# Where matmul operands lie modulo 256 bytes: one place for all moving and stationary tiles, and 64 and 192 bytes from it for the gates' weights

## The chip, the core and the metric

The kernel runs on one core of one Trainium2 chip. The metric is device time in microseconds. Before the change the median of three runs is 1592.05 us (1591.93 to 1592.51). TensorE is called PE, its weight loads PEld, VectorE DVE, ScalarE ACT, GpSimd POOL.

## The reference

One layer of a decoder trunk, 512 tokens, width 2048, float32. Conditioning gives shift, scale and gate; the normalised input goes through one wide projection; its parts feed a latent attention of 16 heads and a chunked gating unit; both are gated, added and projected back.

```python
mod = c_act @ w_ada[l] + b_ada[l]
shift, scale, gate = jnp.split(mod, 3, axis=-1)
h = rmsnorm(x, attn_norm_g[l]) * (1.0 + scale[:, None]) + shift[:, None]
proj = h @ w_in[l]
q_lat, kv_lat, k_rope, z_mla, u, v, z_sgu, g_mla, g_sgu = split_cols(proj, IN_SPLITS)
q = (rmsnorm(q_lat, q_norm_g[l]) @ w_uq[l])      # 16 heads of 128 + 64 rotary
kv = (rmsnorm(kv_lat, kv_norm_g[l]) @ w_ukv[l])  # 16 heads: keys 128, values 128
y_mla = causal_mla_attention(q_nope, q_rope, k_nope, k_rope, v_mla) * jax.nn.silu(z_mla)
y_sgu = chunked_causal_sgu(u, v, sgu_norm_g[l], w_spatial[l], b_spatial[l]) * jax.nn.silu(z_sgu)
merged = jax.nn.sigmoid(g_mla) * y_mla + jax.nn.sigmoid(g_sgu) * y_sgu
x = x + gate[:, None] * (merged @ w_out[l])
return rmsnorm(x, final_norm_g)
```

## The kernel before

Every large product is made of three matmuls. A float32 operand is split into a high part (ACT copies it into the type float32r) and a low part (DVE subtracts the high part), and `mm3` (L135) adds high·high (L136), high·low (L137) and low·high (L138). A matmul has a stationary operand of 128 x 128, which a weight load brings into the array, and a moving operand of 128 rows and up to 512 columns. Both are read from SBUF, where a tile has the same address in all partitions. Where a tile starts modulo 256 bytes is called its place here.

The stages, in order:

- Latents (11 to 156 us): the query and key-value latents and three columns of the last head. A stream of weights passes through three raw buffers; `Stream.split_to` (L90) splits each of them into the pairs w0h, w0l and w1h, w1l in turn. Stationary: w. Moving: h, the normalised input, transposed, 16 tiles of high and low parts, 512 columns. A weight gives 24 matmuls.
- v (156 to 340 us): v and the shared rotary key. Stationary: h. Moving: w, 512 columns twice, then 384 twice and 320.
- Gates (351 to 1117 us): z, g, u, s and t (the five gate-like projections) of head pairs. Two products are computed as seven smaller ones, in the manner of Winograd's form of Strassen's algorithm, from sums of weights and of input tiles (s1, s2, s4 are such sums, s3 goes back into h). A slot is one of these: eight column blocks of three matmuls with 256 moving columns (L1255 high·high, L1256 high·low, L1257 low·high), 24 in all, 266 slots. Stationary: w0, w2, w1 in turn, where w0 and w1 are the stream's buffers and w2 (with the raw buffers raw4 to raw7) lies in a pool `c1` on the other side of SBUF. Moving: h, or s1, s2, s4. A planner places ACT, DVE and transfer work of the slots by costs; it budgets 2.53 us of DVE for a slot. Some sums of weights are made by transfers that add while they land; POOL issues those (L636).
- Attention (1117 to 1400 us): for each head query, key and value products from the latents (w stationary for queries and keys with 512 columns, w moving for values with 256), scores, softmax, transposes and the product with the values.
- Output (1400 to 1581 us): merged tiles (b high, g low) stationary, w_out moving with 512 columns; six weights of the last column group are kept as dh and dl; the last block is cut into two of 256 columns.

What sets the places before: the stream's pair tiles are longer than the weights by `HALF` = 16 words, and the caller's `off` says by how much the high part is shifted (the low part gets `HALF - off`). Constants ahead of them in the pool, an `edge` tile on the right side, and `gap` tiles ahead of s1 and behind s4 shift the rest. In the slots' `split` (L651 to L654) the low part alone is shifted by 16 words in w0 and w1, and nothing in w2.

Of the kernel before, what the change touches and what calls it, by code (L numbers as in the profile page):

```python
# [11 lines left out]
F32 = mybir.dt.float32  # L12
F32R = mybir.dt.float32r
# [3 lines left out]
ALU = mybir.AluOpType  # L17
# [3 lines left out]
P = 128  # L21
# [6 lines left out]
SCALE = 1.0 / math.sqrt(192.0)  # L28
NEG = -1.0e30
GW = 1024  # L30
HALF = 16
TYPES = "zgust"


# [25 lines left out]
class Stream:  # L60
# [9 lines left out]
        self.n_dma = self.n_split = 0  # L70
        self.before = {}

    def add(self, ap, n, to=None, off=HALF):
        self.src.append((ap, n, to, off))
        return len(self.src) - 1

# [14 lines left out]
    def split_to(self, i):  # L91
        i = min(i, len(self.src) - 1)
        while self.n_split <= i:
            k = self.n_split
            self.dma_to(k)
            _, n, to, off = self.src[k]
            raw = self.raw.pop(k)
            self.n_split += 1
            if to is not None:
                hi, lo = to()  # L100
            else:
                pool, tag = self.parts[self.next_part]
                self.next_part = (self.next_part + 1) % len(self.parts)
                hi, lo = (pool.tile([P, GW + HALF], F32R, tag=tag + e, name=f"{tag}{e}_{k}")[:, o:o + GW]
                          for e, o in (("h", off), ("l", HALF - off)))
            self.nc.scalar.copy(hi[:, :n], raw[:, :n])  # L106
            self.nc.vector.tensor_tensor(out=lo[:, :n], in0=raw[:, :n], in1=hi[:, :n].bitcast(F32), op=ALU.subtract)  # L107
            self.hl[k] = (hi, lo)
# [8 lines left out]
def trunk_layer(ctx, tc, xT, xn, c, vecs, pos, wada, w1, w2, wv, wv3, wv4, wh, wh15, wq, wqr, wk, wvv, wo, wsT, bsp, gfin, out,  # L117
                dbg=None):
    nc = tc.nc
# [15 lines left out]
    def mm3(ps, ah, al, bh, bl, start, stop):  # L135
        PE.matmul(ps, ah, bh, start=start, stop=False)  # L136
        PE.matmul(ps, ah, bl, start=False, stop=False)  # L137
        PE.matmul(ps, al, bh, start=False, stop=stop)  # L138
# [5 lines left out]
    def pool(name, side=LEFT, **kw):  # L144
        return tc.tile_pool(name=name, bufs=1, side=side, reuse_waits="tile", **kw)
# [11 lines left out]
    def nt(p, shape, dt, tag, **kw):  # L157
        uid[0] += 1
        return p.tile(shape, dt, tag=tag, name=f"{tag}_{uid[0]}", **kw)

    def bcast(src, n):
# [4 lines left out]
    cst = ctx.enter_context(pool("cst"))  # L166
    wp = ctx.enter_context(pool("w"))
    edge = ctx.enter_context(pool("edge", side=RIGHT))
    nt(edge, [P, 24 + HALF], F32, "edge")
    latp = Scope("lat", side=RIGHT)  # L170
    ws = Stream(nc, [(wp, f"wraw{i}") for i in range(3)], [(wp, f"w{i}") for i in range(2)])

# [6 lines left out]
    DVE.memset(one, 1.0)  # L179
    ident = nt(cst, [P, P], F32, "ident")  # L180
    make_identity(nc, ident)
    tri = nt(cst, [P, P], F32, "tri")
    nc.gpsimd.memset(tri, 1.0)
    nc.gpsimd.affine_select(out=tri, in_=tri, compare_op=ALU.is_ge, fill=0.0, base=0,
                            pattern=[[1, P]], channel_multiplier=-1)
    ones = nt(cst, [P, P], F32R, "ones")
    DVE.tensor_copy(ones, one.broadcast_to([P, P]))
    eps = nt(cst, [P, 1], F32, "eps")
# [45 lines left out]
    gq, gr, gk, gvv = {}, {}, {}, {}  # L234
    c1 = [None]
# [2 lines left out]
    gr[0] = ws.add(wqr[0], 768)  # L238
    gq[0] = ws.add(wq[0], 768)
    gk[0] = ws.add(wk[0], 512)  # L240
    gvv[0] = ws.add(wvv[0], 1024, off=0)
    for h in range(1, H):
        gq[h] = ws.add(wq[h], 768)
        if h % 2 == 1 and h + 1 < H:
            gr[(h + 1) // 2] = ws.add(wqr[(h + 1) // 2], 768)
        gk[h] = ws.add(wk[h], 512)
        if h % 2 == 0:
            gvv[h // 2] = ws.add(wvv[h // 2], 1024, off=0)
    dp = [None]
    dlast = []  # L250

    def last_tiles():
        k = len(dlast)
        dlast.append((nt(dp[0].p, [P, GW], F32R, f"dh{k}"),
                      nt(dp[0].p, [P, GW + (HALF if k == 5 else 0)], F32R, f"dl{k}")[:, :GW]))
        return dlast[-1]

    go = {}
    for cg in range(3):
        for i in range(8):  # L260
            go[cg, i] = ws.add(wo[cg, i], GW, off=0)
            if cg == 2 and i < 6:
                go[3, i] = ws.add(wo[3, i], GW, to=last_tiles)
    for i in (6, 7):
        go[3, i] = ws.add(wo[3, i], GW, off=0)
    pend = []

    def get(i, ahead=1, run=1):
        r = ws.get(i, ahead)
        fs, pend[:] = pend[:run], pend[run:]  # L270
        for f in fs:
            f()
        return r
# [11 lines left out]
    def bank():  # L285
        n_bank[0] += 1
        return bank_at(ring[(n_bank[0] - 1) % len(ring)])
# [49 lines left out]
    hh, hl, hx = [None] * KC, [None] * KC, [None] * KC  # L337
# [32 lines left out]
    for q, sl in enumerate(quarters):  # L370
# [4 lines left out]
                            pattern=[[-1, P]], channel_multiplier=1)  # L375
# [26 lines left out]
    def dot_to(n):  # L402
        nonlocal n_dot
        while n_dot < min(n, KC):
            ada_dot(n_dot)
            n_dot += 1
# [82 lines left out]
    def store(dst, src):  # L489
        made.append((dst, src))  # L490
# [20 lines left out]
    for cg, w in enumerate(VW):  # L511
        psv = [bank()[:, :w] for _ in range(4)]
        for i in range(8):
            g = cg * 8 + i
            wH, wL = get(gv[g], ahead=1)
            if g < 8:
                fix_to(FIXED[KC + g], lambda: dot_to(DOTS[KC + g]))
            for k in range(2):
                j = 2 * i + k
                sl = slice(k * w, (k + 1) * w)  # L520
                for n in range(NB):
                    tk = slice(n * P, (n + 1) * P)
                    mm3(psv[n], hh[j][:, tk], hl[j][:, tk], wH[:, sl], wL[:, sl], j == 0, j == KC - 1)
            for j in gate_step.get(g, ()):
                ada_dot(2 * KC + j)
            if g == 31:
                ada.close()
                c1[0] = Scope("c1", side=RIGHT)
                sums["s4"] = nt(c1[0].p, [P, 8, 2, 256], F32R, "s4")
                nt(c1[0].p, [P, HALF], F32, "gap")  # L530
                sums["s4h"], sums["s4l"] = sums["s4"][:, :, 0], sums["s4"][:, :, 1]
            for f in early.pop(g, ()):
                f()
            stores()
        if cg == 0:
            xp.close()
            s12 = Scope("s12")
            nt(s12.p, [P, HALF], F32, "gap")
            for n in ("s1h", "s1l", "s2h", "s2l"):
                sums[n] = nt(s12.p, [P, 8, 256], F32R, n)  # L540
            tb = Scope("tB")

        def evac_v(n, cg, ps):
            m = VW[cg] // P
            w, c0 = m * P, sum(VW[:cg])
            junk = nt(tb.p, [P, S], F32, f"t{n % 2}") if cg == 0 else nt(latp.p, [P, S], F32, f"lat{10 + n % 2}")
            ACT.activation(junk[:, :w], ps[:, :w], AF.Square, accum_out=ssv[:, n, cg:cg + 1])
            t = nt(tb.p, [P, S], F32, "sig", bufs=2)
            ACT.copy(t[:, :VW[cg]], ps[:, :VW[cg]])
            store(v_d[n][:, c0:c0 + w], t[:, :w])  # L550
            if cg == 4:
                store(kr_d[n], t[:, w:VW[cg]])

        for n in range(NB):
            pend.append(lambda n=n, cg=cg, ps=psv[n]: evac_v(n, cg, ps))
# [63 lines left out]
    base = [slot_of[k][1] for k in range(n_pairs)]  # L619
# [27 lines left out]
    def add(k, q, r):  # L647
        tt(raws[k, q], raws[k, q], raws[k, r], ALU.add)

    def split(s):  # L650
        p, k = order[s]  # L651
        src = raws[k, {1: 11, 6: 11, 2: 11, 4: 11, 3: 12, 7: 22, 5: 21}[p]]
        pl, tag = parts[s % 3]
        own = pl is wp  # L654
        hi = nt(pl, [P, GW + (HALF if own else 0)], F32R, tag + "h")[:, :GW]
        lo = nt(pl, [P, GW + HALF], F32R, tag + "l")[:, HALF if own else 0:][:, :GW]
        split_of[s] = hi, lo
        ACT.copy(hi, src)  # L658
        return hi, lo, src
# [417 lines left out]
    used, s_, n = [s_bias] * 3, s_bias + 1, 0  # L1077
# [136 lines left out]
    for s in range(-4, 0):  # L1214
        done[0] = s
        if s % 2 == 0:
            half = (s + 4) // 2
            wH, wL = get(gz[half], ahead=1 if half == 0 else 0, run=0)
        for f in pend[:2]:
            f()  # L1220
        del pend[:2]
        if s == -1:
            while pend:
                pend.pop(0)()
            tb.close()
            mis = Scope("more")
            sg[0] = Scope("sgu")
        run(s, FIRST, EVAC, GATE)
        if s == -4:
            plain = bank_at(plain_bank)  # L1230
        for k in range(4):
            j = (s + 4) * 4 + k
            sl = slice(j % 8 * P, (j % 8 + 1) * P)
            mm3(plain, wH[:, sl], wL[:, sl], hh[j], hl[j], j == 0, j == KC - 1)
        run(s, SPLIT, BACK, MISC, LOAD)
        stores()
# [342 lines left out]
    for n in range(NB):  # L1579
# [16 lines left out]
        y, o = yt[:, n], 1536 + o  # L1596
# [80 lines left out]
```

## Time and profile before

| | before |
|---|---|
| median of three runs | 1592.05 us |
| profiled execution | 1591.48 us, span 1589.8 us |
| PE busy | 1575.8 us, 99% of the span, 10728 matmuls |
| PEld busy | 1462.7 us, 92% |
| DVE, ACT, POOL busy | 72%, 47%, 6% |
| TensorE clock granted | 1.00 nearly throughout |
| gates, 351 to 1117 us | 6384 of the matmuls, PEld busy 99% |

A matmul is pipelined: the next one starts before it ends, so the durations in the rows (277 ns, say) are longer than the time from start to start. In the timeline the first column is an instruction's start in us from the start of the span, the second its duration. In a table of stretches the columns are named in its first row. In a group of instructions (the page's fifth part) the columns are line, engine, operation, output<-inputs (moving, then stationary), shapes, count | busy us, mean ns | idle time ahead and what ended it.

### The profile page before, as it was taken

The numbers are of one execution on the slowest core, as the hardware profiler recorded it, in microseconds if no ns is written. First come the engines' busy times: TensorE is split into PE (matmuls) and PEld (weight loads), VectorE is DVE, ScalarE is ACT, GpSimd is POOL, SyncE is SP. The second block draws the span as 40 slices with busy tenths as digits, with TensorE's granted clock in tenths as the row PEclk, the third lists the DMA queues.
The fourth block names the chain that finished last, engine by engine and source line by source line (L and its number), as shares of the span: only waits on it lengthen the run. The fifth ranks groups of instructions, "written<-read, shape, count | busy, mean of one in ns | idle before, by whom it ended". The sixth has DMA issues, their size and how long they took to land.

```text
span 1589.8 us, 26944 instructions
## 1 busy us (share of the span) xinstructions
PE 1575.8 (99%) x10728; PEld 1462.7 (92%) x10728; DVE 1151.0 (72%) x1665; ACT 749.9 (47%) x1291; POOL 88.8 (6%) x110
## 2 busy tenths in 40 slices
PE   9999999999999999999999999999999999999997
PEld 7888889999999999999999999999888888888886
DVE  8889669848777777766767777766777877854443
ACT  4443333454545454454555646555655555532322
POOL 0000000001111111111111101012000000000000
PEclk9999999999999999999999999999999999999999
DMA  9978489567888988887778787788422323245422
GB/s 379 363 283 309 164 279 313 201 202 186 235 239 234 249 224 233 239 216 185 195 210 242 213 242 225 212 217 218 140 83 88 102 90 96 88 155 190 132 80 106
DMA packets 120174, 320.21 MB, mean 201 GB/s; under 512 B 13784, under 2 KB 35312, under 8 KB 113264
## 3 DMA queue, kind: packets, MB, share of 16 engines
q1 hardware_dynamic: 104768, 269.72, 49.3%
q0 software_dynamic: 15280, 48.77, 17.2%
q8 instruction: 84, 1.38, 0.4%
q14 instruction: 42, 0.34, 0.1%
HBM read 294.51 MB, written 23.93 MB: 200 GB/s over the span
## 4 chain that ended last, share of the span: by engine, by line
PE 94%; DVE 2%; DMA 1%; ACT 1%; issue 1%; SPq 0%; DVEq 0%; ACTq 0%
PE ps L136 15%; PE ps L137 15%; PE ps L138 15%; PE ps L1256 15%; PE ps L1255 15%; PE ps L1257 15%; PE ps L1434 1%; PE ps L832 1%; PE ps L1398 1%; PE ps L1397 1%; DMA wraw<-in_w 1%; DVE w2l L124 0%; DVE wraw L124 0%; DMA half<-in_pos 0%; DMA kr_d<-sig 0%
## 5 line engine op out<-in xcount | busy, mean ns | idle before, releaser
L107 DVE TENSOR_TENSOR w0l<-wraw,w0h 128x1024 fp32r<-128x1024 f32 (+3 forms) x74 | 79.0, 1068 | 65.6 <-ACT w0h L106 64.8
L106 ACT CAST w0h<-wraw 128x1024 fp32r<-128x1024 f32 (+3 forms) x74 | 69.0, 932 | 112.4 <-PE ps L138 69.8
L106 ACT CAST w1h<-wraw 128x1024 fp32r<-128x1024 f32 (+3 forms) x74 | 63.7, 861 | 120.5 <-PE ps L138 62.6
L107 DVE TENSOR_TENSOR w1l<-wraw,w1h 128x1024 fp32r<-128x1024 f32 (+3 forms) x74 | 73.1, 988 | 60.3 <-ACT w1h L106 59.4
L1255 PE MATMUL ps<-h,w0h 128*128 128x256 f32 x416 | 115.3, 277 | 0.9 <-DVE lat L124 0.9
L1256 PE MATMUL ps<-h,w0h 128*128 128x256 f32 x416 | 115.3, 277 | 0.0
L1257 PE MATMUL ps<-h,w0l 128*128 128x256 f32 x416 | 115.1, 277 | 0.0
L1256 PE MATMUL ps<-h,w1h 128*128 128x256 f32 x400 | 113.0, 283 | 0.0
L1255 PE MATMUL ps<-h,w1h 128*128 128x256 f32 x400 | 112.2, 281 | 0.0
L1255 PE MATMUL ps<-h,w2h 128*128 128x256 f32 x400 | 112.1, 280 | 0.0
L1256 PE MATMUL ps<-h,w2h 128*128 128x256 f32 x400 | 111.5, 279 | 0.0
L1257 PE MATMUL ps<-h,w1l 128*128 128x256 f32 x400 | 111.5, 279 | 0.0
L1257 PE MATMUL ps<-h,w2l 128*128 128x256 f32 x400 | 111.4, 278 | 0.0
L127 DVE SCALAR_TENSOR_TENSOR wada<-wada,cact 128x2048 f32<-128x2048 f32 x47 | 107.1, 2281 | 0.0
L124 DVE TENSOR_TENSOR w2l<-raw,w2h 128x1024 fp32r<-128x1024 f32 x56 | 68.5, 1224 | 35.2 <-ACT w2h L658 34.8
L136 PE MATMUL ps<-w0h,h 128*128 128x256 f32 (+3 forms) x288 | 93.3, 324 | 0.0
L138 PE MATMUL ps<-w0h,h 128*128 128x256 f32 (+3 forms) x288 | 92.9, 322 | 0.0
L137 PE MATMUL ps<-w0l,h 128*128 128x256 f32 (+3 forms) x288 | 92.7, 322 | 0.1
L136 PE MATMUL ps<-h,w1h 128*128 128x512 f32 x226 | 90.1, 399 | 0.0
L137 PE MATMUL ps<-h,w1h 128*128 128x512 f32 x226 | 88.5, 392 | 0.4 <-DVE h L127 0.4
L138 PE MATMUL ps<-h,w1l 128*128 128x512 f32 x226 | 88.2, 390 | 0.0
L124 DVE TENSOR_TENSOR w0l<-wraw,w0h 128x1024 fp32r<-128x1024 f32 x43 | 52.6, 1223 | 38.5 <-ACT w0h L658 38.4
(343 smaller groups left out, 5296.3 us busy)
## 6 DMA issues: line engine op xcount, KB each, us to landing
raw<-in_wh SPq DMA_DIRECT2D x105, 512.0 KB, 5.3
wada<-in_wada SPq DMA_DIRECT2D x47, 1024.0 KB, 7.4
wraw<-in_wh POOLq DMA_DIRECT2D x55, 512.0 KB, 6.9
wraw<-in_wh SPq DMA_DIRECT2D x45, 512.0 KB, 8.0
raw<-in_wh POOLq DMA_DIRECT2D x36, 512.0 KB, 8.9
wraw<-in_wo SPq DMA_DIRECT2D x32, 512.0 KB, 3.7
half<-in_w SPq DMA_DIRECT2D x35, 256.0 KB, 5.0
wraw<-in_w SPq DMA_DIRECT2D x16, 512.0 KB, 8.4
```

The lines of the kernel that those rows point to most:

```text
L106: self.nc.scalar.copy(hi[:, :n], raw[:, :n])
L107: self.nc.vector.tensor_tensor(out=lo[:, :n], in0=raw[:, :n], in1=hi[:, :n].bitcast(F32), op=ALU.subtract)
L124: DVE.tensor_tensor(out=out, in0=in0, in1=in1, op=op)
L127: DVE.scalar_tensor_tensor(out=out, in0=in0, scalar=scalar, in1=in1, op0=op0, op1=op1, **kw)
L136: PE.matmul(ps, ah, bh, start=start, stop=False)
L137: PE.matmul(ps, ah, bl, start=False, stop=False)
L138: PE.matmul(ps, al, bh, start=False, stop=stop)
L832: PE.matmul(ps[:, n], v[:, n], wr[:, q], start=True, stop=True)
L1255: PE.matmul(ps[:, :256], wH[:, cols[c]], xh, start=c == 0 and first, stop=False, skip_group_check=True)
L1256: PE.matmul(ps[:, :256], wH[:, cols[c]], xl, start=False, stop=False, skip_group_check=True)
L1257: PE.matmul(ps[:, :256], wL[:, cols[c]], xh, start=False, stop=c == 7, skip_group_check=True)
L1397: PE.matmul(ps, q2[:, q], krh[:, :n], start=False, stop=False)
```

## The change

`HALF` goes. The stream's tiles get fixed lengths, 48 words more for a high part and 16 for a low one, and each use names where in them its parts begin: `SAME` = (0, 16), `GATES` = (16, 0), `VALUES` = (48, 0) words of 4 bytes. The 48 and 16 words make each pair's base the same modulo 256 whichever of the pairs it is. In the pool of w2 the tiles are 32 and 16 words longer with no shift, which gives it the places of w0 and w1. The triangular mask `tri` (512 bytes per partition) leaves the constants for a later pool on the left side, the `edge` tile is 16 words shorter, the gap ahead of s1 goes, and dl5 needs no padding.

The places in the built programs, bytes modulo 256, moving / stationary:

| stage | before | after |
|---|---|---|
| latents | h 64 / w0 192, w1 64 | 128 / 128 |
| v | w0 192, w1 64 / h 64 | 128 / 128 |
| gates, moving | h 64; s1, s2, s4 192 | all 128 |
| gates, stationary, high and low | w0 128, 0; w1 0, 128; w2 0, 0 | all three 192, 64 |
| query and key products | 64 / w0 192, w1 64 | 128 / 128 |
| value products (all by w0) | high 128, low 0 / 64 | 64, 64 / 128 |
| scores, softmax·v | 64 / 64 | 128 / 128 |
| output | w0 128, 0; w1 0, 128; dh, dl 0 / 128 | 128 / 128 |
| mixing in the gating unit | 192 / 64 | 128 / 128 |
| transposes of the softmax | 192 / 64 | 192 / 128 |

The raw buffers raw4 to raw7 move from 0 to 192, the other raw buffers stay at 128, and tiles that only DVE and ACT use move by multiples of 32 bytes.

```diff
-HALF = 16
+SAME, GATES, VALUES = (0, 16), (16, 0), (48, 0)
+PAD = (48, 16)
...
-    def add(self, ap, n, to=None, off=HALF):
+    def add(self, ap, n, to=None, off=SAME):
...
-                hi, lo = (pool.tile([P, GW + HALF], F32R, tag=tag + e, name=f"{tag}{e}_{k}")[:, o:o + GW]
-                          for e, o in (("h", off), ("l", HALF - off)))
+                hi, lo = (pool.tile([P, GW + pad], F32R, tag=tag + e, name=f"{tag}{e}_{k}")[:, o:o + GW]
+                          for e, pad, o in zip("hl", PAD, off))
...
-    nt(edge, [P, 24 + HALF], F32, "edge")
+    nt(edge, [P, 24], F32, "edge")
...
-    tri = nt(cst, [P, P], F32, "tri")
-    nc.gpsimd.memset(tri, 1.0)
-    nc.gpsimd.affine_select(out=tri, in_=tri, compare_op=ALU.is_ge, fill=0.0, base=0,
-                            pattern=[[1, P]], channel_multiplier=-1)
...
-    gvv[0] = ws.add(wvv[0], 1024, off=0)
+    gvv[0] = ws.add(wvv[0], 1024, off=VALUES)
...
-            gvv[h // 2] = ws.add(wvv[h // 2], 1024, off=0)
+            gvv[h // 2] = ws.add(wvv[h // 2], 1024, off=VALUES)
...
-        dlast.append((nt(dp[0].p, [P, GW], F32R, f"dh{k}"),
-                      nt(dp[0].p, [P, GW + (HALF if k == 5 else 0)], F32R, f"dl{k}")[:, :GW]))
+        dlast.append((nt(dp[0].p, [P, GW], F32R, f"dh{k}"), nt(dp[0].p, [P, GW], F32R, f"dl{k}")))
...
-            go[cg, i] = ws.add(wo[cg, i], GW, off=0)
+            go[cg, i] = ws.add(wo[cg, i], GW)
...
-        go[3, i] = ws.add(wo[3, i], GW, off=0)
+        go[3, i] = ws.add(wo[3, i], GW)
...
-                nt(c1[0].p, [P, HALF], F32, "gap")
+                nt(c1[0].p, [P, GATES[0]], F32, "gap")
...
-            nt(s12.p, [P, HALF], F32, "gap")
...
-        own = pl is wp
-        hi = nt(pl, [P, GW + (HALF if own else 0)], F32R, tag + "h")[:, :GW]
-        lo = nt(pl, [P, GW + HALF], F32R, tag + "l")[:, HALF if own else 0:][:, :GW]
+        off, pad = (GATES, PAD) if pl is wp else ((0, 0), (32, 16))
+        hi, lo = (nt(pl, [P, GW + n], F32R, tag + e)[:, o:o + GW] for e, n, o in zip("hl", pad, off))
...
             mis = Scope("more")
+            tri = nt(mis.p, [P, P], F32, "tri")
+            nc.gpsimd.memset(tri, 1.0)
+            nc.gpsimd.affine_select(out=tri, in_=tri, compare_op=ALU.is_ge, fill=0.0, base=0,
+                                    pattern=[[1, P]], channel_multiplier=-1)
```

On PE, ACT, DVE and in SP's queue every instruction keeps its position. Only POOL's order changes. POOL before, from the masks at the program's start to the first adding transfers of the gates:

```order
masks.py:199 AFFINE_SELECT ident_76<-ident_76 128x128
L183 MEMSET tri_81 128x128
L184 AFFINE_SELECT tri_81<-tri_81 128x128
L189 MEMSET eps_86 128x1
L374 AFFINE_SELECT mask_70<-mask_70 128x128
L636 DMA raw_269_2982<-in_wh 128x1024
L636 DMA raw_268_2980<-in_wh 128x1024
```

The same place in the changed kernel:

```order
masks.py:199 AFFINE_SELECT ident_76<-ident_76 128x128
L186 MEMSET eps_83 128x1
L370 AFFINE_SELECT mask_70<-mask_70 128x128
L1222 MEMSET tri_3071 128x128
L1223 AFFINE_SELECT tri_3071<-tri_3071 128x128
L631 DMA raw_267_2978<-in_wh 128x1024
L631 DMA raw_266_2976<-in_wh 128x1024
```

The two instructions that make `tri` have moved from the start to a position behind the causal mask's and ahead of the first adding transfer; they wait there for DVE, which used their space before.

## The prediction

> **What bounds the kernel now.** I read the page first, then the time by stage, then matmul starts in the timeline. The page:
>
> ```profile
> span 1589.8 us, 26944 instructions
> PE 1575.8 (99%) x10728; PEld 1462.7 (92%) x10728; DVE 1151.0 (72%) x1665; ACT 749.9 (47%) x1291; POOL 88.8 (6%) x110
> PE 94%; DVE 2%; DMA 1%; ACT 1%; issue 1%; SPq 0%; DVEq 0%; ACTq 0%
> ```
>
> TensorE is busy for 99% of the span and carries 94% of the chain that ended last. The kernel is one row of 10728 matmuls, so the time is their number times the pitch, by which I mean the time from one matmul's start to the next one's. A change that alters no matmul can help only through the pitch. By stage (stretch, its length, then busy time and count of each engine, clock, DMA share, GB/s):
>
> ```profile
> core 0: us, PE busy (x) PEld busy (x) DVE busy (x) ACT busy (x) POOL busy (x), PEclk, DMA share, GB/s
> 10.66:99.60 88.94, 88.55 (x384) 72.08 (x384) 80.19 (x96) 38.21 (x54) 0.00 (x0) 1.00 0.90 353
> 100.30:155.85 55.55, 55.55 (x242) 45.31 (x241) 50.69 (x63) 19.26 (x27) 0.00 (x0) 1.00 0.84 313
> 155.85:244.20 88.35, 88.35 (x385) 72.06 (x384) 61.42 (x76) 30.65 (x45) 0.00 (x0) 1.00 0.67 229
> 244.20:311.90 67.70, 67.70 (x385) 66.83 (x385) 61.15 (x94) 25.43 (x52) 0.00 (x0) 1.00 0.77 267
> 351.10:1117.40 766.30, 763.80 (x6534) 762.03 (x6533) 568.07 (x696) 398.47 (x586) 86.13 (x99) 1.00 0.82 220
> 1117.40:1400.20 282.80, 282.50 (x1630) 249.20 (x1629) 223.01 (x477) 157.54 (x383) 0.00 (x0) 1.00 0.31 99
> 1425.00:1565.00 140.00, 140.00 (x607) 113.59 (x606) 63.56 (x81) 41.28 (x60) 0.00 (x0) 1.00 0.42 144
> ```
>
> The gates (351 to 1117) are half of the kernel, and there the weight loads too are busy all the time (762 of 766). In no stage does the clock fall below 1.00, so a pitch that varies isn't the throttle. And it varies, in instructions of one shape:
>
> ```profile
> L1255 PE MATMUL ps<-h,w0h 128*128 128x256 f32 x416 | 115.3, 277 | 0.9 <-DVE lat L124 0.9
> L1256 PE MATMUL ps<-h,w1h 128*128 128x256 f32 x400 | 113.0, 283 | 0.0
> ```
>
> The same product from the same h is 6 ns shorter from w0 than from w1. What differs is where the tiles lie (the table of places): measured from the moving tile, w0's high part lies 64 bytes on and its low part 192; for w1 it is 192 and 64; for w2, 192 and 192. With s1, s2, s4 the first two change roles, and w2 has 64 and 64. Starts in the timeline (start, us, instruction), first rows of slots mostly:
>
> ```profile
> 661.12 0.28 PE L1255 MATMUL ps<-h,w1h 128*128 128x256 f32 x1
> 663.97 0.28 PE L1255 MATMUL ps<-h,w0h 128*128 128x256 f32 x1
> ...
> 680.82 0.28 PE L1255 MATMUL ps<-h,w0h 128*128 128x256 f32 x1
> 683.56 0.28 PE L1255 MATMUL ps<-h,w2h 128*128 128x256 f32 x1
> ...
> 686.28 0.28 PE L1255 MATMUL ps<-s2h,w1h 128*128 128x256 f32 x1
> ...
> 689.01 0.28 PE L1255 MATMUL ps<-h,w0h 128*128 128x256 f32 x1
> 689.13 0.28 PE L1256 MATMUL ps<-h,w0h 128*128 128x256 f32 x1
> 689.25 0.28 PE L1257 MATMUL ps<-h,w0l 128*128 128x256 f32 x1
> 689.37 0.28 PE L1255 MATMUL ps<-h,w0h 128*128 128x256 f32 x1
> 689.49 0.28 PE L1256 MATMUL ps<-h,w0h 128*128 128x256 f32 x1
> 689.60 0.28 PE L1257 MATMUL ps<-h,w0l 128*128 128x256 f32 x1
> ...
> 691.75 0.28 PE L1255 MATMUL ps<-s1h,w2h 128*128 128x256 f32 x1
> ...
> 694.58 0.28 PE L1255 MATMUL ps<-h,w1h 128*128 128x256 f32 x1
> ...
> 697.43 1.05 PE L832 MATMUL ps<-wsr,lat 128*128 128x128 f32 x8
> 698.24 0.36 PE L1255 MATMUL ps<-s,w0h 128*128 128x256 f32 x1
> 698.45 0.28 PE L1256 MATMUL ps<-s,w0h 128*128 128x256 f32 x1
> ```
>
> A slot is 24 matmuls. (64, 192), in the order high, low: h with w0, 680.82 to 683.56 and 689.01 to 691.75, 2.74 us or 114.2 ns each; s2 with w1, 686.28 to 689.01, 2.73. (192, 64): h with w1, 661.12 to 663.97, 2.85 us or 118.8. (64, 64): s1 with w2, 691.75 to 694.58, 2.83 or 117.9. The other slots fall into the same classes; a few poor ones are fast behind a restart, as the one from 698.24.
>
> The third thing to see is inside the slot from 689.01: it begins at 0.12 a matmul, and from the fourth on (689.37, 689.49, 689.60) it falls to 0.113 and stays: (691.75 − 689.49)/20 = 113.0. The (64, 192) slots find this pace from any start and hold it. The w2 slot from 683.56, at (192, 192), follows such a slot and keeps the pace it was handed: 2.72/24 = 113.3. So the pace has memory: a good place locks it, a poor one at best doesn't spoil it.
>
> The same with 512 columns, in the latents:
>
> ```profile
> 22.50 0.40 PE L136 MATMUL ps<-h,w0h 128*128 128x512 f32 x1
> ...
> 28.09 0.39 PE L136 MATMUL ps<-h,w1h 128*128 128x512 f32 x1
> ...
> 33.55 0.40 PE L136 MATMUL ps<-h,w0h 128*128 128x512 f32 x1
> ```
>
> w0 lies 128 bytes from h: 5.59/24 = 232.9 ns. w1 lies at h's own place: 5.46/24 = 227.5, its first four or so still recovering from w0; settled it is 226.7, twice 113.3.
>
> **The change part by part.** No matmul, copy or transfer of data is added or removed. The places move: distance 0 for the latents, v, query and key products, scores and output; (64, 192) for every gate slot, whichever weight or moving tile; (64, 64) for the value products.
>
> Gates. 766.30 us less some 15 for the 150 other matmuls (eight in 698.24 − 697.43, 0.10 each) and some 6 at 30 restarts (0.21 instead of 0.12 at 698.24, a few far longer) leave 745 for 6384 matmuls: 116.7 ns. If a slot behaves as a (64, 192) slot does now, 114.2; if the lock is never given up, since no slot follows a poor one, 113.3. I take 113.6, near the lock, because the slow rows stand at the start of a slot that follows another distance or a restart, and only the restarts remain: 6384 × 3.1 = 19.8 us. Ends: 16.0 (114.2) and 21.7 (113.3); below nothing if the lock fails (rivals).
>
> Latents. 312 of 624 matmuls from 232.9 to 226.9 and 312 from 227.5 to 226.9: 2.1 us, with the two blocks at 340 us 2.2. v: 88.35/384 = 230.1, to 226.9, 1.2 us; at 384 columns 67.70/384 = 176.3, where I credit 0.5. Output: 140.00 us over 605 starts (two more run in from before) is 231.4; there each product mixes distances 0 and 128; 720 × (231.4 − 227.2) = 3.0. If that stage stays at 229, 1.7. Query and key: 624 matmuls, half of them from w0, but broken by attention work, so they re-lock each time: 312 × 2.7 to 6, 0.8 to 1.9; I take 1.2. Scores and softmax·v are at distance 0 before and after: nothing.
>
> Value products, 384 matmuls, go from 192 and 64 in turn to (64, 64):
>
> ```profile
> L136 PE MATMUL ps<-w0h,h 128*128 128x256 f32 x128 | 36.6, 286 | 0.0
> ```
>
> 286 is in the poor group's manner and (64, 64) reads 117.9 above, so 0 to 384 × 5 = 1.9 us if they inherit a lock; I take 0.3.
>
> Feeders. What could swallow a shorter slot is whoever feeds it. DVE works 568 of 766 us (74%, then 76%), DMA 0.82 (then 0.84), and PE's waits in the gates now are few:
>
> ```profile
> PE ps L1255 <- ACT lat L773: 1.0, 1, 1.0
> PE ps L1255 <- DVE lat L124: 0.9, 1, 0.9
> ```
>
> Both are single waits. I give back 1 us. In the latents DMA is at 0.90 and DVE at 80 of 89 us, but the gain there is 1 us over 16 steps; a missing cover would cost that 1 us.
>
> The triangle. Two POOL instructions move:
>
> ```profile
> 1.93 0.66 POOL L184 TENSOR_SCALAR_AFFINE_SELECT tri<-tri 128x128 f32<-128x128 f32 x1
> ...
> 350.65 0.98 POOL L636 DMA_DIRECT2D raw<-in_wh  x1 [340.84 <-DVE raw L124]
> ```
>
> They cost under 0.9 us and now stand ahead of the first adding transfer, after 340 us of idle POOL. They wait for DVE's last use of the pool whose space they take:
>
> ```profile
> 309.72 0.42 DVE L124 TENSOR_TENSOR s2l<-t,s2h 128x256 fp32r<-128x256 f32 x1
> ```
>
> That is 40 us before the transfer. If they were late, the transfer at 350.65 would be late by at most that 0.9; I cost it at nothing.
>
> Sum: 19.8 + 2.2 + 1.7 + 3.0 + 1.2 + 0.3 − 1.0 = 27 us. The profiled execution took 1591.48 (span 1589.8), so 1564.5; the runs' median lies 0.57 above it: **1565**.
>
> A rule against the change: the Trainium skill, "TensorE: Matmul & The Clock Gate", Step-by-step, says that TensorE has "two independent read ports", one for the moving and one for the stationary operand. By it the relative place of the two could not matter, and the result would be 1592 (last but one of the rivals). The 277 against 283 above doesn't agree.
>
> **The rivals.** (1) Partial: each class keeps its present average; slot edges unlock it again. Gates 16.0, latents 312 × 5.4 = 1.7, v 1.0, output 1.7, query and key 0.8: 21.2, less the same 1: 1591.48 + 0.57 − 20.2, hence **1572**. For it: every (64, 192) slot now begins with slow rows. Against: the one before always had another distance or another absolute place.
>
> (2) The feeders bind: a slot of 2.72 us leaves DVE, ACT and transfers less room, and one slot in three waits 0.1 us: 266/3 × 0.1 = 9 back, **1574**. For it: 0.82 DMA; against: the waits above.
>
> (3) Two operands don't disturb each other and the 6 ns come from something that goes along with the buffers' turn, their writers for instance: **1592**. Against it: w1 is slow with h and fast with s2, in the same turn.
>
> (4) Slower: the lock depends on the absolute place. Moving tiles lie at 64 or 192 now and never, in the gates, at 128. If (128; high 192, low 64) acts as the mirrored class does, all gate slots go to 119.0: 6384 × 2.3 = 14.7 lost, less 7.5 gained elsewhere: **1599**. It decides from the pitch at which the gates lose 7.5 us, 117.9. Against: 64 and 192 give one result for one distance, so a shift by 128 is free; only a shift by 64 is untested.
>
> That the allocator misses the places is excluded: the table of places is the built program's.
>
> **How the numbers follow.** Forecast 0.62, partial 0.18, feeders 0.10, no effect 0.04, slower 0.06. The forecast's own range is 1559 to 1569 (gates locked at 113.3 and value products locked, or output and queries at their low ends). The range for 8 in 10 reaches over the partial case and most of the feeders': 1557 to 1576. Within 0.2% (3.2 us, about what runs of this kernel can tell) counts as the same: faster 0.90, same 0.04, slower 0.06.
>
> **What would show it.** Right: all gate slots of 2.72 to 2.73 us whatever w0, w1, w2 and h or s; slow rows only behind a restart; w0 blocks in the latents at 5.45 us; the gate stage near 747 us. Partial: slots of 2.74. Feeders: new PE waits for DVE or ACT rows of L124 and L658. Wrong: slots of 2.83 or more, or w0 and w1 still apart.

## The result and the profile after

| | before | after | ratio, 95% interval |
|---|---|---|---|
| median, first comparison (4 runs each) | 1592.18 us (1591.93 to 1592.51) | 1564.62 us (1563.93 to 1568.05) | 0.9831 (0.9814 to 0.9848) |
| median, second comparison (9 and 5 runs) | 1592.19 us | 1563.93 us (1563.72 to 1565.06) | 0.9823 (0.9809 to 0.9837) |

Faster by 28 us. Two executions far outside are left out of the ratios and ranges here and below: one of the kernel before (2138 us, at a granted clock of 0.68) and one of the kernel with one moving place and three distances (7367 us).

The profile of the first comparison fell on its slowest execution, 1568.05 us with a span of 1566.3. Its page, with the same rows as the prediction showed of before (L1253 to L1255 are the gates' three products now, formerly L1255 to L1257; in the same way `mm3`'s L136 to L138 are L137 to L139 now):

```profile
span 1566.3 us, 26945 instructions
PE 1548.8 (99%) x10728; PEld 1443.3 (92%) x10728; DVE 1148.9 (73%) x1665; ACT 749.3 (48%) x1291; POOL 88.7 (6%) x110
PE 89%; DVE 5%; DMA 2%; ACT 2%; issue 1%; SPq 0%; DVEq 0%; ACTq 0%
L1253 PE MATMUL ps<-h,w0h 128*128 128x256 f32 x416 | 115.3, 277 | 1.2 <-DVE lat L125 1.2
L1253 PE MATMUL ps<-h,w1h 128*128 128x256 f32 x400 | 111.8, 280 | 0.0
L1254 PE MATMUL ps<-h,w1h 128*128 128x256 f32 x400 | 111.2, 278 | 0.0
```

The same 10728 matmuls, 27 us less of PE, and the row of L1254 with w1 reads 278 ns where the same product read 283. The other engines do what they did, to 2 us of DVE.

An execution of the second comparison (1563.98 us, span 1562.3) is the one to compare with the prediction's stage table. Its stretches hold the same instructions; columns as there:

```profile
core 0: us, PE busy (x) PEld busy (x) DVE busy (x) ACT busy (x) POOL busy (x), PEclk, DMA share, GB/s
10.80:99.00 88.20, 87.40 (x384) 71.92 (x385) 80.12 (x96) 38.35 (x54) 0.00 (x0) 1.00 0.91 356
154.50:241.50 87.00, 87.00 (x385) 72.05 (x384) 61.35 (x76) 30.68 (x45) 0.00 (x0) 1.00 0.68 233
241.50:309.00 67.50, 67.50 (x386) 66.47 (x385) 61.29 (x94) 25.49 (x52) 0.76 (x2) 1.00 0.76 268
348.00:1095.10 747.10, 743.79 (x6535) 742.03 (x6535) 566.33 (x696) 398.13 (x586) 86.13 (x99) 1.00 0.83 226
1095.10:1375.90 280.80, 280.48 (x1629) 248.90 (x1629) 222.72 (x477) 157.20 (x383) 0.00 (x0) 1.00 0.31 100
1400.00:1540.00 140.00, 140.00 (x619) 115.91 (x619) 63.34 (x81) 41.37 (x60) 0.00 (x0) 1.00 0.43 148
```

The gates take 747.10 us instead of 766.30, v's 512-column part 87.00 instead of 88.35, and 140 us of the output hold 619 matmuls instead of 607. The clock is 1.00 as before. Starts in the same execution, six rows of the gates and three first rows of latent blocks:

```profile
27.09 0.39 PE L137 MATMUL ps<-h,w0h 128*128 128x512 f32 x1
32.53 0.39 PE L137 MATMUL ps<-h,w1h 128*128 128x512 f32 x1
37.97 0.39 PE L137 MATMUL ps<-h,w0h 128*128 128x512 f32 x1
...
678.05 0.28 PE L1253 MATMUL ps<-h,w0h 128*128 128x256 f32 x1
680.77 0.28 PE L1253 MATMUL ps<-s1h,w2h 128*128 128x256 f32 x1
683.49 0.28 PE L1253 MATMUL ps<-h,w1h 128*128 128x256 f32 x1
686.21 1.05 PE L826 MATMUL ps<-wsr,lat 128*128 128x128 f32 x8
687.02 0.37 PE L1253 MATMUL ps<-s,w0h 128*128 128x256 f32 x1
...
689.88 0.28 PE L1253 MATMUL ps<-h,w2h 128*128 128x256 f32 x1
```

Latent blocks of w0 and w1 take 5.44 us alike (5.59 and 5.46 before). A slot takes 2.72 us with w0, w2 or w1 and with h or s: (680.77 − 678.05)/24 = 113.3 ns from its first matmul on. Only the slot behind the restart at 687.02 is longer, 2.86 us, and the next is back at the pace. A restart is a slot that begins behind other matmuls or a wait, or has a wait inside. Counted by pauses of more than 130 ns from one start to the next, 237 of the 266 slots have none ahead of them or inside, and all of these run at 113.3 to 113.4 on average; behind the stage's first start and the 28 restarts the pace comes back within the slot.

Two of PE's waits in the gates in this execution (line, what it waited for: us, times, longest), and the one that is in the slower profile alone (last row, from the first comparison):

```profile
PE ps L1253 <- ACT lat L767: 1.4, 2, 1.1
PE ps L1253 <- DVE lat L125: 1.2, 1, 1.2
```

```profile
PE ps L1120 <- DMA half<-kr_d: 2.0, 1, 2.0
```

The first profile lies 3.4 us above its median. That much, 3.5 us, it spends more in waits in the gates' stretch than this one, 2.0 of them on this one transfer, at the same pitch (113.49 ns); they did not come again.

### The profile page after: what moved, and what is told of

Same layout as the page of the kernel before. It is cut to its first block, busy times and chain, and to the rows that moved or that the text cites. A ratio compares the mean times of both kernels' runs of the same rounds, so it can differ in the third digit from the quotient of the medians.

```text
span 1566.3 us, 26945 instructions
## 1 busy us (share of the span) xinstructions
PE 1548.8 (99%) x10728; PEld 1443.3 (92%) x10728; DVE 1148.9 (73%) x1665; ACT 749.3 (48%) x1291; POOL 88.7 (6%) x110
## 4 chain that ended last, share of the span: by engine, by line
PE 89%; DVE 5%; DMA 2%; ACT 2%; issue 1%; SPq 0%; DVEq 0%; ACTq 0%
PE ps L138 14%; PE ps L139 14%; PE ps L137 14%; PE ps L1253 14%; PE ps L1255 14%; PE ps L1254 14%; PE ps L1432 1%; PE ps L826 1%; DVE wada L128 1%; DMA latn_d<-half 1%; DVE t L125 1%; DMA wraw<-in_w 1%; PE ps L1396 1%; PE ps L1395 1%; DMA half<-kr_d 1%
## 5 line engine op out<-in xcount | busy, mean ns | idle before, releaser
L1253 PE MATMUL ps<-h,w0h 128*128 128x256 f32 x416 | 115.3, 277 | 1.2 <-DVE lat L125 1.2
L1255 PE MATMUL ps<-h,w0l 128*128 128x256 f32 x416 | 115.1, 277 | 0.0
L1254 PE MATMUL ps<-h,w0h 128*128 128x256 f32 x416 | 115.0, 277 | 0.0
L1253 PE MATMUL ps<-h,w1h 128*128 128x256 f32 x400 | 111.8, 280 | 0.0
L1255 PE MATMUL ps<-h,w1l 128*128 128x256 f32 x400 | 111.2, 278 | 0.0
L1254 PE MATMUL ps<-h,w1h 128*128 128x256 f32 x400 | 111.2, 278 | 0.0
L1253 PE MATMUL ps<-h,w2h 128*128 128x256 f32 x400 | 111.2, 278 | 0.0
L1255 PE MATMUL ps<-h,w2l 128*128 128x256 f32 x400 | 110.6, 277 | 0.0
L1254 PE MATMUL ps<-h,w2h 128*128 128x256 f32 x400 | 110.6, 277 | 0.0
L137 PE MATMUL ps<-w0h,h 128*128 128x256 f32 (+3 forms) x288 | 92.8, 322 | 0.0
L138 PE MATMUL ps<-w0l,h 128*128 128x256 f32 (+3 forms) x288 | 92.5, 321 | 0.1
L139 PE MATMUL ps<-w0h,h 128*128 128x256 f32 (+3 forms) x288 | 92.2, 320 | 0.0
L137 PE MATMUL ps<-h,w1h 128*128 128x512 f32 x226 | 89.8, 398 | 0.1
L138 PE MATMUL ps<-h,w1h 128*128 128x512 f32 x226 | 88.3, 391 | 0.8 <-DVE h L128 0.8
L139 PE MATMUL ps<-h,w1l 128*128 128x512 f32 x226 | 88.2, 390 | 0.0
```

Of the source, the lines that this page charges most:

```text
L1253: PE.matmul(ps[:, :256], wH[:, cols[c]], xh, start=c == 0 and first, stop=False, skip_group_check=True)
L1254: PE.matmul(ps[:, :256], wH[:, cols[c]], xl, start=False, stop=False, skip_group_check=True)
L1255: PE.matmul(ps[:, :256], wL[:, cols[c]], xh, start=False, stop=c == 7, skip_group_check=True)
```

## The experiments

The three kernels of series (m1_map, m2_fine, m3_sizes_restarts) leave the layer out: they copy x to the output and run matmuls of one size at chosen places, with no other engine at work. The five others compute the whole layer. In all tables pitches are in ns, start to start, of undisturbed matmuls; distances are (high, low) as in the prediction. "Restart" and "without a break" are counted as above.

### A map of distances

```diff
+    for n, mh, ml, sh, sl in CONFIGS:      # mh, ml: places of the moving parts; sh, sl: of the stationary ones
+        block(n, *BAD[n], 4)               # 12 matmuls at a poor distance
+        block(n, mh, ml, sh, sl, 16)       # 48 at the tried one: high·high, high·low, low·high
```

> The layer itself is left out: input rows are copied to the output, and TensorE runs 208 series of matmuls on one tile, each of 12 matmuls at a poor distance and 48 at the distance that is tried (three per column block as in the kernel: stationary high with moving high, stationary high with moving low, stationary low with moving high). Places of moving low, stationary high and stationary low relative to moving high go through 0, 64, 128, 192 for 256, 384 and 512 moving columns. My theory (the distance of the stationary from the moving tile modulo 256 sets whether the pitch settles at its floor): at 256 columns with both moving parts at one place, stationary (64, 192) settles at 113.3 ns within a dozen matmuls after the poor start, (192, 64) stays near 119, (64, 64) and (192, 192) near 117.8, (0, 0) near 119 to 120 as in the attention; at 512 columns (0, 0) settles at 226.7 and (128, 128) stays near 232.7. Rival (uniformity: any place settles if nothing changes it): every series of a shape settles at one pitch. Rival (ports are independent and the 6 ns come from other engines' accesses): with no other engine at work all series have the floor from their first matmul.

Measured over the last 24 of each series, both moving parts at one place:

| columns | distances and pitch |
|---|---|
| 256 | (64, 192) 113.3; (64, 64) 113.3; (0, 0) 120.0; (192, 64) 118.9; (192, 192) 117.8; the other eleven 116.7 to 118.9 |
| 512 | (0, 0) 226.7; (192, 192), (192, 0) and (192, 64) 228.9; (64, 64) 233.3; the others 230.0 to 233.5 |
| 384 | (0, 0), (192, 192) and three others 173.3; up to 176.7 |
| 320 | all four tried 146.7 |

With the two moving parts at different places the best are 115.5 (256), 227.8 (512), 171.1 (384) and 144.4 (320).

So the pitch follows the places with nothing else running: the rival that put the 6 ns down to the buffers' writers falls, and so does the one by which any place settles if nothing changes it. On this grid of 64 bytes nothing beats the change's choices for 256 and 512 columns. The same distance isn't good for both: 0 is the best for 512 and the worst of its row for 256. One thing didn't fit: the 12 poor matmuls at (192, 64) ran at 113.3 to 114.4 ahead of many of the series and at 118.7 to 119.5 ahead of others.

### Finer steps, and the whole arrangement moved

```diff
+CONFIGS = [(256, 0, 0, 0, d, -d % 256) for d in E]                       # E: 0, 16, ... 240
+CONFIGS += [(n, 0, 0, 0, d, d) for n in (256, 384, 512) for d in E]
+CONFIGS += [(256, 0, a, a, (a + 64) % 256, (a + 192) % 256) for a in E]   # (64, 192), everything moved by a
+CONFIGS += [(512, 0, a, a, a, a) for a in E]                             # distance 0, everything moved by a
+CONFIGS += [(256, 1, 0, 0, sh, sl) for sh in Q for sl in Q]              # 1: behind 12 matmuls at a good distance
+CONFIGS += [(512, 1, 0, 0, s, s) for s in Q]                             # Q: 0, 64, 128, 192
```

> The layer itself is left out, as in the map. Distances in steps of 16 bytes at 256, 384 and 512 columns, the whole arrangement shifted in steps of 16 bytes, and series that start from a good distance instead of a poor one. My theory: a shift of everything changes nothing (113.3 for (64, 192) and 226.7 for 0 at every shift); after a good start (192, 192), (64, 64) and (192, 64) hold 113.3 for a while or for all 48 matmuls, where after a poor start they stay at 117.8 to 119. Rival (absolute place): the shifted series differ, best at 128. Rival (no memory): the start makes no difference. For the distances between multiples of 64 I have no rows; if the lock needs an exact distance only few of the 16 settle.

Four series of 256 columns, the 25th and the 48th matmul of each: distance (0, 0); (64, 192); (64, 192) with everything moved by 16 bytes; the same by 32 bytes.

```profile
60.41 0.28 PE L49 MATMUL b<-T 128*128 128x256 f32 x1
63.17 0.28 PE L51 MATMUL b<-T 128*128 128x256 f32 x1
...
88.66 0.28 PE L49 MATMUL b<-T 128*128 128x256 f32 x1
91.26 0.28 PE L51 MATMUL b<-T 128*128 128x256 f32 x1
...
683.56 0.28 PE L49 MATMUL b<-T 128*128 128x256 f32 x1
686.27 0.28 PE L51 MATMUL b<-T 128*128 128x256 f32 x1
...
690.50 0.28 PE L49 MATMUL b<-T 128*128 128x256 f32 x1
693.11 0.28 PE L51 MATMUL b<-T 128*128 128x256 f32 x1
```

Divided by 23: 120.0, 113.0, 117.8 and 113.5. The full result: of the sixteen distances (d, −d) only 64 and 192 reach 113.3, of the sixteen (d, d) only 64 and 192; the others lie at 116.7 to 120.2. For 512 columns (d, d) gives 226.7 at 0 and 16 and 228.3 to 234.5 elsewhere. Moved by a multiple of 32 bytes, all eight arrangements find 113.3, and 226.7 with 512 columns. Moved by an odd multiple of 16, none does: 117.6 to 117.9 and 230.0 to 233.3.

The absolute place counts, then, but only in steps finer than any that this change makes. And (192, 64) and (192, 192) stood at 113.3 here, where the map had 118.9 and 117.8: one distance, two paces.

The series behind a good start say which distances can hold a pace that they are handed. With 256 columns, behind 12 matmuls at (64, 192), the distances (192, 64), (64, 64) and (192, 192) stay at 113.3 over all 48 matmuls, as (64, 192) itself does; the other twelve settle at 115.6 to 120.0. With 512 columns no such memory shows: behind a good start the distances 64, 128 and 192 settle at 233.3, 232.1 and 228.9, just as they did in the map behind a poor one.

### The gates mirrored

```diff
         hi, lo = (nt(pl, [P, GW + n], F32R, tag + e)[:, o:o + GW] for e, n, o in zip("hl", pad, off))
+        hi, lo = lo, hi
```

Every gate slot then has (192, 64), with one moving place.

> The changed kernel, but the high parts of the gates' weights lie at distance 192 and the low parts at 64, in all slots alike. My theory: the slots lose the lock at the first restart and stay near 119.0, so the gates take 6384 x 5.5 ns = 35 us more than in the changed kernel: 1600, slower than before the change. Uniformity alone: the gates stay at 113.5 and the time at 1564 to 1566. Absolute place (what helps is that moving tiles lie at 128): also 1564 to 1568.

Measured: 1589.10 us (1584.29 to 1590.70, 9 runs), ratio 0.9976 (0.9966 to 0.9986). 24 to 25 us slower than the changed kernel, so the direction is right and the size isn't. First rows of slots in its profiled execution (1585.27 us; high parts are named l here):

```profile
483.45 0.28 PE L1254 MATMUL ps<-h,w1l 128*128 128x256 f32 x1
486.17 0.28 PE L1254 MATMUL ps<-s1h,w0l 128*128 128x256 f32 x1
488.89 0.28 PE L1254 MATMUL ps<-h,w2l 128*128 128x256 f32 x1
...
504.80 0.28 PE L1254 MATMUL ps<-h,w0l 128*128 128x256 f32 x1
507.66 0.28 PE L1254 MATMUL ps<-s1h,w2l 128*128 128x256 f32 x1
510.51 0.28 PE L1254 MATMUL ps<-h,w1l 128*128 128x256 f32 x1
```

Slots of 2.72 us (113.3 ns) ahead of two restarts at 492 and 499 us, of 2.85 to 2.86 (118.9) behind them, at one and the same distance. Over the whole stage 94 slots run at 113 to 114 and 172 at 119. In 238 steps from slot to slot without a break the state never changed; of the stage's first start and 27 restarts, 10 left it fast and 18 slow. The theory that a distance has a pace of its own falls. (192, 64) has two steady states, and a restart decides between them. That fits the spread of this kernel's times, 6 us, where the changed kernel's, but for the one disturbed by waits, spread over 1.3; only one execution was profiled, so it isn't shown.

### The gates alone

```diff
-SAME, GATES, VALUES = (0, 16), (16, 0), (48, 0)
-PAD = (48, 16)
+SAME, GATES, VALUES = (0, 32), (16, 16), (16, 16)
+PAD = (32, 32)
...
+                off = (32, 0) if off is SAME and tag == "w0" else off
...
```

The gates keep the new places; in latents, v, query and key products and output w0 lies 128 bytes from its partner again, and the value products' parts lie 64 and 192 bytes from theirs.

> The changed kernel, but in the stream's other uses w0 lies 128 bytes from the place that w1 and the other operand share, as before the change in the latents, v, query and key products (and for the output's w0), and the value products have 192 and 64 in turn. My theory: the gates keep 113.5; the latents' and v's w0 blocks go back from 226.8 to 232.7 and their w1 blocks to 227.4; together with output and queries 6.5 to 8 us more than the changed kernel: 1571 to 1573. If the gates' gain hung on one place for the whole kernel, the gates would lose it too: 1590.

Measured: 1571.49 us (1570.68 to 1573.88), ratio 0.9875 (0.9859 to 0.9892). Stretches of gates and output:

```profile
351.20:1098.30 747.10, 743.79 (x6535) 742.08 (x6534) 566.83 (x696) 397.90 (x586) 85.95 (x99) 1.00 0.83 226
1400.00:1540.00 140.00, 140.00 (x611) 114.37 (x611) 64.84 (x79) 41.48 (x59) 0.00 (x0) 1.00 0.43 151
```

The gates take the changed kernel's 747.10 us, the output has lost most of its gain (611 against 619, and 607 before). Of the 28 us, 20.6 remain: 19.2 is the gates' stretch, and about 1 is the output's, where w1 and the kept weights dh and dl stay at the new places. The 7 that are lost were the other stages'.

### The changed kernel again

No edit: the kernel after the change as it stands.

> The changed kernel once more, for a profile to set beside the others of this chip. If its excess of waits in the gates (10.2 us in the first profile, 6.0 before the change) belongs to the change, they come again and the gate stage takes 751 us as before; if it was that one execution, they lie near 6.7 us as in the version that moves the gates alone, and the gate stage takes about 747 us, the span about 1563 us. The time 1563 to 1566 us either way, the ratio 0.982 to 0.984, and 6 to 8 us below the version that moves the gates alone.

Measured: 1563.93 us (1563.72 to 1565.06), and the profile that the result shows: the excess of waits in the gates (what the pauses of the restarts take beyond the pitch) is 6.7 us, against 6.0 before the change and 10.2 in the first profile. Those 3.5 us belonged to one execution.

### One moving place, three distances

```diff
+        off = off if pl is wp else (32, 0)
         hi, lo = (nt(pl, [P, GW + n], F32R, tag + e)[:, o:o + GW] for e, n, o in zip("hl", pad, off))
+        if tag == "w1":
+            hi, lo = lo, hi
```

> The gates' uniformity undone and nothing else: the moving tiles stay at one place, w0 keeps (64, 192), w1 gets its parts the other way round, (192, 64), and w2 both parts at 192 bytes from the moving tile: before the change these are the three classes that meet h, here they meet every moving tile. Theory A (each slot has to lie at the one locking distance itself, since a slot at another distance takes up its own pace): w0 slots 114.2 ns a matmul, w1 118 to 119, w2 113.3 to 118 by what precedes; mean 116 to 117, 6384 x 2.7 to 3.3 = 17 to 21 us above the changed kernel, 1582 to 1586 us. Theory B (the two other distances hold what they are handed, and w0 in every third slot hands them the fast pace): w1 and w2 at 113.3 to 114.5 except behind a restart that loses it until the next w0 slot: mean 113.9, 2 to 4 us above, 1567 to 1569 us.

Measured: 1566.19 us (1565.98 to 1566.22), ratio 0.9836 (0.9820 to 0.9851): theory B, a little below its 1567. The distances (192, 64) and (192, 192), slow in most of their slots before the change, cost 2.3 us here. First rows of slots; the first is behind a restart:

```profile
499.27 0.36 PE L1256 MATMUL ps<-h,w2h 128*128 128x256 f32 x1
502.18 0.28 PE L1256 MATMUL ps<-s2h,w1l 128*128 128x256 f32 x1
505.03 0.28 PE L1256 MATMUL ps<-h,w0h 128*128 128x256 f32 x1
507.75 0.28 PE L1256 MATMUL ps<-s1h,w2h 128*128 128x256 f32 x1
510.47 0.28 PE L1256 MATMUL ps<-h,w1l 128*128 128x256 f32 x1
513.19 0.28 PE L1256 MATMUL ps<-s,w0h 128*128 128x256 f32 x1
```

The restart leaves w2 slow (2.91 us with the restart in it) and w1 stays slow (2.85). Then w0 at (64, 192) comes, and from 505.03 on w0, w2 and w1 take 2.72 us each, until the next restart. Handed the fast pace without a break, w2 at (192, 192) kept it in 83 of 83 slots and w1 at (192, 64) in 69 of 69. Handed the slow pace by w2, w1 stayed slow in four slots and found the fast pace by itself in a fifth.

This shows what the trace of before had held. There, a slot at a distance other than (64, 192) that followed a fast slot without a break kept the pace in 12 of 12 cases where the moving tile's place stayed (h behind h, as the slot at 683.56 in the prediction's rows), and lost it in 41 of 41 where it changed (h at 64 to s at 192 or back, as the one at 691.75). But 35 of those 41 lay at (64, 64) and all 12 at (192, 192), so that trace alone can't tell the moving place from the distance; the last experiment can.

### Series: stationary columns, and restarts

```diff
+    for n, m, d in SIZES:                        # 128, 64, 32 stationary columns
+        block(n, *BAD[n], 4)
+        block(n, 0, 0, *d, 16, m)
+    for j, d in RESTARTS:                        # behind j matmuls of 128 moving columns, j = 1 to 12
+        ...
+        block(256, 0, 0, *d, 16)
+    for j, d in RESTARTS:                        # behind a wait for DVE
+        ...
+        block(256, 0, 0, *d, 16, base=6144)
```

> The layer is left out; x is copied to the output, and series of matmuls alone are measured. First part: 128, 64 and 32 stationary columns at a fast and at a slow distance, with 256 and 512 moving columns. If the slow distance costs because weight loads and moving reads get in each other's way, the excess (120.0 - 113.3 = 6.7 ns at 256, 233.3 - 226.7 = 6.6 at 512 columns, 128 stationary ones) falls with the number of stationary columns loaded, to about 3.3 and 1.7 ns; the floor, 113.3 and 226.7, which goes with the number of moving columns, stays. If it doesn't come from the loads, the excess stays at 6.7 whatever is loaded. Second part: 48 restarts behind 1 to 12 matmuls of 128 moving columns, and third, 48 restarts behind a wait for another engine, each into one of four distances in turn. If (64, 192) alone finds the fast pace from any start and the three others have two steady states, (64, 192) ends at 113.3 in all 24 restarts, and (192, 64), (64, 64) and (192, 192) end at 113.3 in some and at 117.8 to 118.9 in the others, and never change within a series. If the distances differ in the average alone, each shows one pace.

Restarts that end at 113.3, of 12 (the rest at 117.8 or 118.9):

| distance | behind 128-column matmuls | behind a wait |
|---|---|---|
| (64, 192) | 12 | 12 |
| (192, 64) | 7 | 12 |
| (64, 64) | 9 | 0 |
| (192, 192) | 3 | 0 |

(64, 192) finds the pace within some 3 to 15 matmuls from every start; the three others hold whichever state they have settled in. Behind the wait they settle the same way each time; behind the short matmuls, of which there are 1 to 12, now one way and now the other.

Stationary columns: 256 moving ones at distance (0, 0), 25th and 48th matmul, with 128 and with 64 stationary columns.

```profile
67.56 0.28 PE L49 MATMUL b<-T 128*128 128x256 f32 x1
70.33 0.28 PE L51 MATMUL b<-T 128*128 128x256 f32 x1
...
81.33 0.28 PE L49 MATMUL b<-T 128*64 128x256 f32 x1
83.93 0.28 PE L51 MATMUL b<-T 128*64 128x256 f32 x1
```

2.77/23 = 120 ns and 2.60/23 = 113. With half a weight, and likewise with 32 columns, the excess is gone altogether, neither halved nor kept. With 512 columns and 64 or 32 stationary ones the slow distance (64, 64) stays slow (232.6 and 231.1 instead of 233.3), and the fast one, 0, becomes slower: 230.0 and 231.7 instead of 226.7. So how much is loaded matters, but the simple price per loaded column that I had in mind is not what there is. Part of the cause stays open here.

### One distance for all weights, two moving places

```diff
             s12 = Scope("s12")
+            nt(s12.p, [P, 32], F32, "gap12")
```

s1 and s2 move by 128 bytes; 76 of the 266 slots get (192, 64) and a changing moving place.

> The other half of the gates' arrangement undone: every weight keeps its places, but the moving tiles s1 and s2 (76 of the 266 slots) lie 128 bytes from h and s4, so that these slots have the distances (192, 64) and a moving place that changes ahead of them and behind them. Beside them 64 small products of the gating unit (128 columns) move to distance 128, which can cost 64 x 0.01 = 0.6 us at most. Theory C (what undoes the fast pace is the change of the moving place; a slot at one of the holding distances keeps a handed pace only while the moving place stays): all s1 and s2 slots at 118.7 to 118.9, so 76 x 24 x 5.4 = 9.8 us, and the slots behind them begin slow and find the pace again, 0.5 to 1.5 us: 1574 to 1576 us. Theory B2 (the distance (192, 64) keeps what it is handed in any case, as it did when the weights' places were varied and the moving place stayed): as there, 2 to 4 us, 1566 to 1568 us.

Measured: 1573.87 us (1573.70 to 1574.50), ratio 0.9886 (0.9870 to 0.9903): 9.9 us above the changed kernel, the lower end of theory C (1574 to 1576) and not theory B2 (1566 to 1568). First rows of four slots:

```profile
524.71 0.28 PE L1254 MATMUL ps<-h,w2h 128*128 128x256 f32 x1
527.44 0.28 PE L1254 MATMUL ps<-s1h,w1h 128*128 128x256 f32 x1
530.29 0.28 PE L1254 MATMUL ps<-h,w0h 128*128 128x256 f32 x1
533.02 0.28 PE L1254 MATMUL ps<-s,w2h 128*128 128x256 f32 x1
```

2.73, 2.85, 2.73. All 71 unbroken steps from a fast slot into s1 or s2 lost the pace at the first matmul, all 70 back out of them found it again, within some four matmuls. (192, 64) kept a handed pace in 69 of 69 slots of the kernel with one moving place, and here in none of 71: it is the change of the moving tile's place that undoes it.

## Why the prediction was right, and where its reasons were not

The time was predicted at 1565 and is 1564 to 1565. The four signs that were to show it came: slots of 2.72 us whatever the weight and the moving tile, slow rows behind restarts only, w0 blocks of 5.44 us, a gate stage of 747. By its terms, against the execution with a span of 1562.3 (us, from sums of starts over each stage in both traces):

| term | predicted | measured |
|---|---|---|
| gates, less waits | 19.8 − 1.0 | 19.3 (pitch 116.68 to 113.50: 20.3; waits and restarts take 1.0 more) |
| latents | 2.2 | 1.6 (pitch 2.2, the rest taken by waits) |
| v | 1.7 | 1.6 |
| output | 3.0 | 3.1 |
| query and key | 1.2 | 2.0 (pitch 230.93 to 227.79) |
| value products | 0.3 | 0.0 (117.77, then 117.78) |
| sum | 27 | 27.6 (the spans differ by 27.5) |

**Gates.** That the pace can be locked and that (64, 192) finds it from any start was read from one slot, the one from 689.01, a thin base that turned out right; the pitch of 113.6 came out at 113.50. The reason given for taking 113.6 rather than 114.2, that slow rows stand behind "another distance or a restart", named the wrong half. A change to one of this kernel's other distances loses nothing by itself (83 and 69 slots of the kernel with one moving place). What lost it before was the moving tile's place, which went from 64 to 192 and back. "A poor one at best doesn't spoil it" was too weak as well: with one moving place, (192, 64) and (192, 192) hold the fast pace for as long as nothing breaks it, and mirrored throughout, (192, 64) holds the slow one too. The number was safe because the change does both things, and either alone keeps most of the gain: one moving place and three distances costs 2.3 us of it, one set of weight places and two moving places 9.9.

**Partial (1572).** It needed slot edges to unlock the pace. None of the 237 unbroken edges does.

**Feeders (1574).** Excess waits in the gates went from 6.0 to 6.7 us, with DVE at 76% and transfers at 0.83. Slack was enough; the give-back of 1 us was of the right size.

**No effect (1592).** The series with no other engine show 113.3 against 120.0 by places alone. By the Trainium skill ("TensorE: Matmul & The Clock Gate", Step-by-step) the two operands come through "two independent SBUF read ports". Here moving one against the other changes the pitch by 6.7 ns of 113.3, so the inference that the prediction draws from it, that their relative place can't matter, doesn't hold. Whether it is at the ports that they meet, no run here shows.

**Slower (1599).** A move by 64 or 128 bytes is free, as is any multiple of 32 (both sizes), so the absolute place doesn't turn the sign. Its premise, that the mirrored distance would cost 119.0 in every slot, is wrong too: mirrored throughout, the kernel takes 1589.

**Query and key** was sized too small: I let half of it re-lock after every piece of attention work and took 1.2 of 0.8 to 1.9, and the pitch of all 624 matmuls fell by 3.1 ns all the same, 2.0 us. **Value products** were credited with handed paces and got none (117.8 is the slow pace of (64, 64)); they stand behind other work each time, which fits the 12 of 12 restarts behind a wait that went slow. **Output** came out as summed, but one piece of it was overlooked: the 96 matmuls of the last block have 256 columns, and distance 0, the best for 512, is the slowest of its row in the map for 256. Their pitch rose from 118.4 to 119.9, 0.15 us lost.

**The triangle.** POOL made it at 307 us, 40 us ahead of its first transfer of the gates:

```profile
307.49 0.55 POOL L1223 TENSOR_SCALAR_AFFINE_SELECT tri<-tri 128x128 f32<-128x128 f32 x1
347.54 0.99 POOL L631 DMA_DIRECT2D raw<-in_wh  x1 [39.50 <-DVE raw L125]
```

It cost nothing, as assumed.

What stays open is why. That loads and moving reads disturb each other fits the excess that vanishes with 64 stationary columns at 256, and doesn't fit what 512 columns do; and no run says what it is that a slot hands to the next.

## What to carry to other kernels

When matmuls of one shape show two pitches in a trace, sort them by where their two operands start modulo 256 bytes, and look at the first matmuls after each change: an average over the shape hides states that are handed on. Give all moving tiles of a stage one place first, then put the stationary ones at a distance that finds the fast pace from any start, found by a short series for the column count in use ((64, 192) at 256, 0 at 512 in this scheme of three products). Work out the gain as count times the settled pitch, and expect restarts to cost only their own few matmuls.

## What the runs showed of the hardware that I had not expected

- A pace with memory: at (192, 64), (192, 192) and (64, 64) one and the same sequence of matmuls runs steadily at 113.3 or at 117.8 to 118.9, and what came before decides which. In 238 unbroken steps of the mirrored kernel the state never changed. It shows with 256 columns; the four distances tried with 512 show none.
- The settled pitch is 113.3 with 256 columns and 226.7 with 512, the same 0.4427 ns a column, at full granted clock; no series went below it. 384 and 320 columns had 171.1 and 144.4 at best, 0.4456 and 0.4513 a column.
- Shifting a good arrangement by 16 bytes costs 4.5 ns at 256 columns; by 32, nothing.
- With 64 stationary columns the worst distance for 256 moving ones is as fast as the best; with 512 the best one gets 3.3 ns slower.
